# Layer 1's up projection as seven half-size block products, right operands summed and split once

## The chip, the cores and the metric

One core of a Trainium2 chip runs the whole program. The metric is the device time of one execution in microseconds. The engines are TensorE (PE, matmuls, with weight loads shown apart as PEld), VectorE (DVE), ScalarE (ACT), GpSimd (POOL) and SyncE (SP); here POOL and SP mostly issue DMA transfers. Each engine works off its own queue in order and waits on semaphores for the others.

## The reference

Two layers of a hybrid block over 1024 latent tokens (and 256 context tokens, which layer 1 reads but no longer updates), D = 1024, followed by a final norm. The change touches the feed-forward part of layer 1:

```python
def conv_ffn(h, w_up, conv_w, conv_b, w_down):
    u = dwconv(h @ w_up, conv_w, FFN_CONV // 2) + conv_b      # D_FF = 2816, w_up: D x 2*D_FF, 3 taps over tokens
    gate, val = jnp.split(u, 2, axis=-1)
    return (jax.nn.silu(gate) * val) @ w_down
...
        x = x + g1[:, None, :] * y_l
        x = x + g2[:, None, :] * conv_ffn(modulate(x, norm_ffn_g[layer], sh2, sc2), ffn_w_up[layer], ...)
    return rmsnorm(x, final_norm_g)
```

`modulate` is an RMS norm times (1 + scale) plus shift. Everything is float32.

## The kernel before

Activations lie transposed, channels on the 128 partitions and tokens along the row: x is eight tiles of 128x1024 (`xl`). A float32 product is made of three matmuls of fp32r operands. Each operand is split into a high part (ACT casts it, line 315) and a low part (DVE subtracts, line 316), and `mm3` (line 336) adds high x high, high x low and low x high in PSUM.

A layer is mixers, then `project_out` (the output projection, which adds onto x in two passes, first token half B0 and then B1), then `norm_block` for the two halves, `ffn_up` and `lat_down`. Tiles come from rings: 36 slots of 128x1024 (`L`), 8 of 128x512 (`H2`), two weight slots for raw loads (`wr`, `wd`, one each), two each for their high and low parts (`wh`, `wl`), in PSUM two tiles of two banks (tag a, `ps`) and four of one bank (tag b, `pb1`). A scheduler orders each engine's instructions, mostly in the order of the code, and puts in the waits; what it made of the code is fixed when the program is built.

`ffn_up` walks over 22 chunks of 128 channels, gate then value (`up(f, val)`, line 1260). One block loads 1024x128 weights (`wr`, 512 KB), splits them, and multiplies both token halves (`pu`, 2 x 24 matmuls of 128x512 on line 341). Then the three-tap convolution reads PSUM: ACT applies the middle tap and the bias (line 1275), DVE the two outer taps (1276, 1277). ACT makes Silu of the gate (1280), DVE multiplies (1220). In layer 0 the context tokens are a second job in the same loop (`puc`), with their own down projection `ctx_down` (`pd`, line 1253, added onto `xc`). The products are kept in SBUF (`bt`) or parked in DRAM (`act`, from GpSimd's queue, lines 1223 to 1230).

`lat_down` (line 1303) is already a product in seven block products of half size. Chunks of even and odd number are the two halves of the sum. Its seven stages take six pairs of chunks each, 24 matmuls a pair; operands for the next pair are made while one runs (`operands`, line 1429: `ah`/`al` from raw weight loads, `br`/`bd` or `rb`/`db` from activations `b`). Accumulators are `px` (tag a) and `py` (tag b). At the end of layer 1 `fin` normalises and stores the output.

## Time and profile before

| | |
|---|---|
| three runs | 3070.68, 3074.61, 3086.83 us; median 3074.61 |
| profiled run | 3071.11 us, of which the span 3069.0 |
| PE, DVE, ACT busy | 95%, 57%, 43% of the span |
| layer 1's first up-projection matmul to its last | about 2328 to 2816 us |
| layer 1's down projection to the end | about 2816 to 3069 us |

Times inside the run are microseconds from the span's start. A row of the timeline gives the start, the duration, engine, line, operation, output and input tiles (buffer numbers left out), and in brackets how long the engine sat idle before it and what ended that. "x3" is three such instructions in a row. A window row gives the stretch, then the busy time of each engine with the number of its instructions, the granted clock of PE (1.00 is full), the busy share of the DMA engines and GB/s.

### The profile page before, as it was taken

The page shows a single profiled execution, that of the slowest core. Times are in us where ns is not written, and L with a number is a line of the kernel's source. Part 1 is how long each engine was busy: PE and PEld are TensorE (multiplying, and loading weights), DVE is VectorE, ACT ScalarE, POOL GpSimd, SP SyncE. Part 2 cuts the span into 40 slices and gives each one's busy share as a digit, 9 for nine tenths or more (in the row PEclk, how much of TensorE's full clock was granted, in tenths as well). Part 3 has the DMA queues.
Part 4 walks back from the last instruction along what each step waited for, and adds up shares of the span by engine and source line. Part 5 has one row for each costly group of instructions (what it writes and reads, how often), then busy time and mean ns, then how long its engine had stood idle before and what let it go on. Part 6 is the DMA issues. An engine that isn't in the chain of part 4 may idle for free.

```text
span 3069.0 us, 41616 instructions
## 1 busy us (share of the span) xinstructions
PE 2925.5 (95%) x16472; PEld 2323.1 (76%) x16472; DVE 1764.7 (57%) x2746; ACT 1312.6 (43%) x2219; POOL 184.6 (6%) x284
## 2 busy tenths in 40 slices
PE   6999898989999999999999899998999999999998
PEld 5877675559888888888778787775577888887776
DVE  5466555665644444444686756767755444345775
ACT  5366754663422222222333555766744222223343
POOL 2000011010000000000111000011000000001010
PEclk8999999999999999999999999999999999999998
DMA  7221247333232232221575200123053222123672
GB/s 293 69 63 49 73 125 193 105 112 115 93 97 96 93 100 88 71 76 66 195 255 155 82 28 29 33 78 93 19 164 124 62 62 62 55 62 113 216 196 90
DMA packets 271571, 318.44 MB, mean 104 GB/s; under 512 B 18156, under 2 KB 199568, under 8 KB 271376
## 3 DMA queue, kind: packets, MB, share of 16 engines
q1 hardware_dynamic: 242928, 231.29, 24.2%
q0 software_dynamic: 28272, 84.43, 8.5%
q8 instruction: 130, 2.13, 0.3%
q14 instruction: 65, 0.53, 0.1%
q10 hardware_dynamic: 176, 0.07, 0.0%
HBM read 265.12 MB, written 50.59 MB: 103 GB/s over the span
## 4 chain that ended last, share of the span: by engine, by line
PE 82%; ACT 6%; DVE 6%; DMA 4%; issue 2%; SPq 0%; ACTq 0%; DVEq 0%; POOLq 0%
PE pu L341 31%; PE pl L341 9%; PE px L1457 7%; PE py L1457 4%; PE puc L341 4%; PE iv L587 3%; PE yo L1160 3%; PE sc L1005 3%; PE yo L1154 2%; PE pov L1047 2%; PE pc L341 2%; PE pt L1030 2%; PE pd L1253 2%; PE ada L199 2%; PE hd L668 2%
## 5 line engine op out<-in xcount | busy, mean ns | idle before, releaser
L341 PE MATMUL pu<-hh,wh 128*128 128x512 f32 x1408 | 555.8, 395 | 1.5 <-ACT u L1275 1.3
L341 PE MATMUL pu<-hh,wl 128*128 128x512 f32 x1408 | 552.2, 392 | 0.0
L341 PE MATMUL pu<-hl,wh 128*128 128x512 f32 x1408 | 548.6, 390 | 0.0
L315 ACT CAST wh<-wr 128x1024 fp32r<-128x1024 f32 x154 | 161.5, 1050 | 513.1 <-PE pu L341 277.4
L316 DVE TENSOR_TENSOR wl<-wr,wh 128x1024 fp32r<-128x1024 f32 x154 | 190.0, 1234 | 329.9 <-ACT wh L315 322.7
L341 PEld LDWEIGHTS pu<-hh,wh 128*128 128x128 f32 x1408 | 264.5, 188 | 66.9 <-issue 11.4
L341 PEld LDWEIGHTS pu<-hh,wl 128*128 128x128 f32 x1408 | 264.4, 188 | 60.0 <-issue 0.7
L341 PEld LDWEIGHTS pu<-hl,wh 128*128 128x128 f32 x1408 | 264.4, 188 | 57.8 <-issue 0.5
L1276 DVE SCALAR_TENSOR_TENSOR u<-pu,col_fcb,u 128x1023 f32<-128x1023 f32 x44 | 56.4, 1283 | 327.3 <-ACT u L1275 327.3
L341 PE MATMUL pl<-hh,wh 128*128 128x512 f32 x512 | 211.0, 412 | 2.2 <-ACT wh L315 1.0
L341 PE MATMUL pl<-hh,wl 128*128 128x512 f32 x512 | 206.0, 402 | 1.1 <-DVE wl L316 1.1
L341 PE MATMUL pl<-hl,wh 128*128 128x512 f32 x512 | 205.2, 401 | 0.0
L1275 ACT ACTIVATE u<-pu,col_nf,col_fcw 128x1024 f32<-128x1024 f32 x44 | 53.0, 1206 | 318.9 <-PE pu L341 318.9
L315 ACT CAST ah<-raw 128x512 fp32r<-128x512 f32 x132 | 76.2, 618 | 216.0 <-PE px L1457 102.6
L341 PEld LDWEIGHTS pl<-hh,wh 128*128 128x128 f32 x512 | 96.4, 188 | 35.3 <-issue 14.0
L316 DVE TENSOR_TENSOR al<-raw,ah 128x512 fp32r<-128x512 f32 x132 | 85.9, 688 | 59.5 <-ACT ah L315 56.2
L1011 DVE TENSOR_REDUCE st<-sc 128x1 f32<-128x641 f32 (+2 forms) x144 | 106.7, 745 | 17.1 <-ACT sc L1010 15.5
L341 PEld LDWEIGHTS pl<-hh,wl 128*128 128x128 f32 x512 | 96.5, 188 | 26.0 <-issue 5.1
L1014 ACT ACTIVATE pb<-sc,st 128x641 f32<-128x641 f32 (+2 forms) x144 | 106.3, 739 | 20.6 <-DVE st L1011 17.8
L341 PEld LDWEIGHTS pl<-hl,wh 128*128 128x128 f32 x512 | 96.7, 189 | 23.8 <-issue 6.3
L1277 DVE SCALAR_TENSOR_TENSOR u<-pu,col_fcw,u 128x1023 f32<-128x1023 f32 x88 | 112.8, 1283 | 3.0
L1005 PEld LDWEIGHTS sc<-kc,qt 128*128 128x128 f32 x288 | 44.0, 191 | 80.0 <-ACT pb L1014 35.9
(419 smaller groups left out, 6587.8 us busy)
## 6 DMA issues: line engine op xcount, KB each, us to landing
raw<-in_ffn_w_down_dram SPq DMA_DIRECT2D x220, 256.0 KB
aw<-in_ada_w_dram SPq DMA_DIRECT2D x96, 512.0 KB
wr<-in_ffn_w_up_dram SPq DMA_DIRECT2D x88, 512.0 KB
wr<-in_w_in_dram SPq DMA_DIRECT2D x34, 512.0 KB
wr<-in_w_out_dram SPq DMA_DIRECT2D x128, 128.0 KB
act<-u POOLq DMA_DIRECT2D x55, 256.0 KB, 4.2
b<-act POOLq DMA_DIRECT2D x25, 512.0 KB, 8.1
dr<-in_ffn_w_down_dram SPq DMA_DIRECT2D x22, 512.0 KB
```

What stands on the lines that cost most here:

```text
L199: PE.matmul(out=pt[32 * q:32 * q + 32, h0:h0 + 256], lhsT=cl[:, k, :], rhs=wr[:, q * 256:(q + 1) * 256], start=(i == 0), stop=(i == 2 * KT ...
L315: S.copy(out=hi, in_=raw)
L316: eng.tensor_tensor(out=lo, in0=raw, in1=hi.bitcast(F32), op=sub)
L341: PE.matmul(out=o, lhsT=wl[k] if pi == 2 else wh[k], rhs=hl[k] if pi == 1 else hh[k], start=(k == 0 and pi == 0), stop=(k == nk - 1 and pi ...
L587: PE.matmul(out=po[:, 0:384], lhsT=hh[1 if pi == 1 else 0][k][:, t0:t0 + P], rhs=wiv[k][1 if pi == 2 else 0], start=(k == 0 and pi == 0), ...
L668: PE.matmul(out=pv[64 * hf:64 * hf + 64, ci, :].rearrange("p (h t) -> p h t", h=2), lhsT=kw(ci, hf), rhs=z[:, :, b:b + 64], start=True, st ...
L1005: PE.matmul(out=o_, lhsT=qt[:, hh, :], rhs=k_[:, ksl], start=(pi == 0), stop=(pi == 1 and not ms))
L1011: V.tensor_reduce(out=st[:, 0, c_], in_=sc[:, s0:769], axis=mybir.AxisListType.X, op=ALU.min)
L1014: S.activation(out=pb, in_=sc[:, s0:769], func=AF.Exp, bias=st[:, 0, c_], scale=-1.0, accum_out=st[:, 1, c_])
L1160: PE.matmul(out=o, lhsT=wl[k] if pi == 2 else wh[k], rhs=a[1 if pi == 1 else 0][:, s_], start=False, stop=(ki == 3 and pi == 2), skip_grou ...
L1277: V.scalar_tensor_tensor(out=u[:, 0:n - 1], in0=pu[:, 1:n], scalar=cw(2), in1=u[:, 0:n - 1], op0=mult, op1=add)
L1457: PE.matmul(out=acc[m], lhsT=(al if pi == 2 else ah)[:, i, c_], rhs=(bl if pi == 1 else bh)[:, i, :], start=((isy or si == 0) and j == 0 a ...
```

## The change

Layer 1 leaves `ffn_up` (which is now layer 0's alone) and gets `ffn_up7`. One chunk f is taken as a 2x2 block product: rows are gate and value weights, the sum runs over two halves of D, columns are the two token halves. In a Winograd form this takes seven products of half the sum's length, 12 matmuls each, instead of eight. The products are numbered by their operands:

- left operands, per chunk: 1 and 2 are halves of the gate weights (`ug`), 4 a half of the value weights (`uv`); 5, 6 and 7 use DVE sums of them (`sums`: s1, s2, s3), and 3 uses s2 with a gate half added by an accumulating DMA from GpSimd's queue. Each is split into `sw` when it is made, three products ahead.
- right operands, once for all chunks: `B11`, `B21`, `B22` are normalised activations, `T1` to `T4` sums of them, made in place in x by `norm7` and `sums7` and split into 28 tiles `t7`. x itself is copied to DRAM (`xmid`) before it is overwritten.
- 1, 6, 5 and 3 add up in one half of a PSUM tile `ux`, which ACT copies out to SBUF after each (`cg`, `cv`); 2 goes to its other half and 7 and 4 to `uz`, which DVE adds to the copies. The convolution then reads SBUF.

Products of the activations are all parked in DRAM, (0, 0) too, and `lat_down` loads them back. In both layers the first operands of `lat_down` are now made before the last block of the up projection (`pre_`, `pre`).

```diff
-             for a, b in ((0, 1), (1, 0), (1, 1))} for l in range(DEPTH)]
+             for a in range(2) for b in range(2)} for l in range(DEPTH)]
...
+            if (f, val) == (NF - 1, 1):
+                pre_()
...
+    def norm7(xs, th, l, xm, tb):
...
+            G.dma_start(out=xm[:, k, sl], in_=x_)
+            hm = H2("hm")
+            V.scalar_tensor_tensor(out=hm, in0=x_, scalar=A_, in1=rs[0], op0=mult, op1=mult)
+            S.activation(out=x_, in_=hm, func=AF.Identity, bias=B_)
+            if th == 0:
+                tb["B11" if k < 4 else "B21"].append(both(x_))
...
+        def sums(f):
+            raws[f, "s1"], s4[f], raws[f, "s3"] = H2("s1"), H2("s2"), H2("s3")
+            V.tensor_tensor(out=raws[f, "s1"], in0=half(raws[f, 1], 0), in1=half(raws[f, 1], 1), op=add)
+            a11 = half(raws.pop((f, 0)), 0)
+            V.tensor_tensor(out=s4[f], in0=a11, in1=raws[f, "s1"], op=sub)
+            V.tensor_tensor(out=raws[f, "s3"], in0=a11, in1=half(raws[f, 1], 0), op=sub)
+            if f + 1 < NF:
+                load_g(f + 1)
...
+            split(half(t_, 0), half(t_, 1), raw)
+            ops[f, i] = half(t_, 0), half(t_, 1)
+            if i == 6:
+                G.dma_start(out=k4(raw), in_=cols(f, 0)[:, 4:8], accum_op=add)
+            if i == 4 and f + 1 < NF:
+                load_v(f + 1)
...
+        for f in range(NF):
+            seq += [(f, 6), (f, 7), (f, 5)] + [(f + 1, 1)] * (f > 0) + [(f, 3), (f, 4)] + [(f + 1, 2)] * (f > 0)
...
+        for n_, (f, i) in enumerate(seq):
+            if n_ == 4:
+                yield
+            if todo:
+                opnd(*todo.pop(0))
+            elif (f, i) == (NF - 1, 3):
+                pre()
...
+            for k in range(4):
+                for pi in range(3):
+                    PE.matmul(out=out, lhsT=(al if pi == 2 else ah)[:, k * P:(k + 1) * P], rhs=rhs[k][1 if pi == 1 else 0],
+                              start=(i in (1, 2, 7) and k == 0 and pi == 0), stop=(k == 3 and pi == 2), skip_group_check=True)
...
+            elif i == 5:
+                S.copy(out=half(cv[f], 1), in_=x_)
+                V.tensor_tensor(out=half(cv[f], 1), in0=half(cv[f], 1), in1=cz[f], op=add)
...
+    def sums7(xs, tb, norm):
...
+                t3 = H2("t3")
+                V.tensor_tensor(out=t3, in0=b22, in1=b12, op=sub)
+                V.tensor_tensor(out=b12, in0=b12, in1=b11, op=sub)
+                V.tensor_tensor(out=b11, in0=b12, in1=b22, op=sub)
+                tb["T2"].append(both(b11))
+                tb["T3"].append(both(t3))
+            tb["T1"] += [both(half(xs[k], 1)) for k in range(4)]
...
+        else:
+            n1 = norm7(xl, 1, l, xmid[l], tb)
+            run(n1, 1)
+            next(f_)
+            sums7(xl, tb, n1)
```

On PE, before, in the middle of layer 1's up projection a block is one run of high and low parts of eight tiles h into one `pu` half:

```order
L341 MATMUL pu<-hh_18800,wh 128x512
L341 MATMUL pu<-hl_18808,wh 128x512
L341 MATMUL pu<-hh_18800,wl 128x512
L341 MATMUL pu<-hh_18801,wh 128x512
L341 MATMUL pu<-hl_18809,wh 128x512
```

On PE, after, at the same place, one chunk's product 6 (right operand T2, tiles 19791 to 19845), then two groups of the next chunk's product 1 (B11, 19320 on), then product 5 (T1, 19851 on) into the PSUM half that 6 left:

```order
L1445 MATMUL ux<-t_19791,sw 128x512 x3
L1445 MATMUL ux<-t_19809,sw 128x512 x3
L1445 MATMUL ux<-t_19827,sw 128x512 x3
L1445 MATMUL ux<-t_19845,sw 128x512 x3
L1445 MATMUL ux<-t_19320,sw 128x512 x3
L1445 MATMUL ux<-t_19374,sw 128x512
L1445 MATMUL ux<-t_19851,sw 128x512 x3
L1445 MATMUL ux<-t_19854,sw 128x512 x3
```

Product 1's remaining eight matmuls stand behind product 5. On DVE, before, a chunk of this stage is weight splits, conv passes and products:

```order
L316 TENSOR_TENSOR wl<-wr,wh 128x1024
L1276 SCALAR_TENSOR_TENSOR u<-pu,col_fcw_1009,u 128x1023
L1277 SCALAR_TENSOR_TENSOR u<-pu,col_fcw_1015,u 128x1023
L1220 TENSOR_TENSOR b<-u 128x512
L1220 TENSOR_TENSOR u<-u 128x512
L1229 TENSOR_TENSOR u<-u 128x512
```

On DVE, after, from the second outer tap of the gate to the first weight sum (s, line 1352) of the next chunk but one; `uv` is the split of operand 4, which frees the value weights' buffer:

```order
L1410 SCALAR_TENSOR_TENSOR u<-cg,col_fcw_1027,u 128x1023
L316 TENSOR_TENSOR sw<-s_20909,sw 128x512
L1409 SCALAR_TENSOR_TENSOR u<-cv,col_fcw_1021,u 128x1023
L1453 TENSOR_TENSOR cg<-cg,ux 128x512
L1410 SCALAR_TENSOR_TENSOR u<-cv,col_fcw_1027,u 128x1023
L316 TENSOR_TENSOR sw<-ug,sw 128x512
L1422 TENSOR_TENSOR u<-u 128x1024
L316 TENSOR_TENSOR sw<-uv,sw 128x512
L1424 TENSOR_TENSOR ev<-u,ev 128x512
L316 TENSOR_TENSOR sw<-s_20910,sw 128x512
L1352 TENSOR_TENSOR s_21050<-uv 128x512
```

The next value load (SP's queue) thus stands behind both conv chains, and the first sum behind that load. On ACT, before, at the start of layer 1's stage the last normalisation passes of the second token half are followed by the weights' cast and the first conv:

```order
L286 ACTIVATE hh_18806<-hm,mod_91 128x512
L286 ACTIVATE hh_18807<-hm,mod_91 128x512
L315 CAST wh<-wr 128x1024
L1275 ACTIVATE u<-pu,col_fcb_995,col_fcw_1009 128x1024 x2
```

On ACT, after, at that place, the last six of the casts of T1, B22 and T4 and what follows them; the first `COPY cv` empties product 6 of chunk 0, the second product 5:

```order
L315 CAST t_19869<-x_18802 128x512
L315 CAST t_19872<-x_18803 128x512
L315 CAST t_19879<-x_18800 128x512
L315 CAST t_19882<-x_18801 128x512
L315 CAST t_19885<-x_18802 128x512
L315 CAST t_19888<-x_18803 128x512
L1457 COPY cv<-ux 128x512
L315 CAST sw<-uv 128x512
L1459 COPY cv<-ux 128x512
```

All twelve casts of those operands stand ahead of the copy.

## Rows read from the trace of the kernel before

**Rows 1.** Page: engines' busy time; the chain that ended last, by engine.

```profile
PE 2925.5 (95%) x16472; PEld 2323.1 (76%) x16472; DVE 1764.7 (57%) x2746; ACT 1312.6 (43%) x2219; POOL 184.6 (6%) x284
...
PE 82%; ACT 6%; DVE 6%; DMA 4%; issue 2%; SPq 0%; ACTq 0%; DVEq 0%; POOLq 0%
PE pu L341 31%; PE pl L341 9%; PE px L1457 7%; PE py L1457 4%; PE puc L341 4%; PE iv L587 3%; PE yo L1160 3%; PE sc L1005 3%; PE yo L1154 2%; PE pov L1047 2%; PE pc L341 2%; PE pt L1030 2%; PE pd L1253 2%; PE ada L199 2%; PE hd L668 2%
```

**Rows 2.** Windows of layer 1's up projection, and the turn behind it.

```profile
2400.00:2500.00 100.00, 100.00 (x438) 82.04 (x438) 42.30 (x41) 24.68 (x23) 2.14 (x4) 1.00 0.19 58
...
2818.00:2830.00 12.00, 7.55 (x22) 5.52 (x23) 8.38 (x9) 2.49 (x4) 5.20 (x9) 0.72 0.59 178
```

**Rows 3.** Timeline of ACT in that stage: two weight casts that follow each other.

```profile
2508.74 1.05 ACT L315 CAST wh<-wr 128x1024 fp32r<-128x1024 f32 x1 [5.01 <-PE pu L341]
...
2519.73 1.05 ACT L315 CAST wh<-wr 128x1024 fp32r<-128x1024 f32 x1 [8.83 <-PE pu L341]
```

**Rows 4.** Groups by line and shape: busy us, mean ns, idle us before.

```profile
L316 DVE TENSOR_TENSOR al<-raw,ah 128x512 fp32r<-128x512 f32 x132 | 85.9, 688 | 59.5 <-ACT ah L315 56.2 <-PE fo L1476 3.1
...
L315 ACT CAST ah<-raw 128x512 fp32r<-128x512 f32 x132 | 76.2, 618 | 216.0 <-PE px L1457 102.6 <-PE py L1457 98.4 <-PE pu L341 11.3
L1034 ACT COPY pts<-pt 128x512 f32<-128x512 f32 x128 | 74.4, 585 | 15.3 <-PE pt L1030 15.3
...
L1275 ACT ACTIVATE u<-pu,col_fcb,col_fcw 128x1024 f32<-128x1024 f32 x44 | 52.8, 1200 | 1.5 <-PE pu L341 1.5
...
L1174 DVE SCALAR_TENSOR_TENSOR x<-yo,mod,x 128x512 f32<-128x512 f32 x32 | 24.0, 750 | 60.5 <-PE yo L1160 60.5
...
L848 DVE SCALAR_TENSOR_TENSOR th<-rg,th 128x1024 f32<-128x1024 f32 x8 | 9.8, 1225 | 9.0 <-ACT rg L889 9.0
```

**Rows 5.** Timelines of PE, then DVE, where layer 1's up projection starts.

```profile
2327.79 0.39 PE L1160 MATMUL yo<-yh,wl 128*128 128x512 f32 x1
2333.03 1.09 PE L270 MATMUL pm<-sq,cft 128*128 128x512 f32 x2 [1.87 <-DVE sq L268]
2354.87 0.47 PE L341 MATMUL pu<-hh,wh 128*128 128x512 f32 x1 [1.34 <-ACT u L1275]
...
2338.13 2.08 DVE L285 SCALAR_TENSOR_TENSOR hm<-x,acol,rs 128x512 f32<-128x512 f32 x3
2358.11 0.69 DVE L1220 TENSOR_TENSOR u<-u 128x512 f32<-128x512 f32 x1
2358.72 1.22 DVE L316 TENSOR_TENSOR wl<-wr,wh 128x1024 fp32r<-128x1024 f32 x1
```

**Rows 6.** Timeline of PE at the turn to layer 1's down projection.

```profile
2816.17 0.40 PE L341 MATMUL pu<-hh,wl 128*128 128x512 f32 x1
...
2823.72 0.79 PE L1457 MATMUL px<-bd,ah 128*128 128x512 f32 x1 [1.61 <-DVE bd L316]
...
2827.30 0.46 PE L1457 MATMUL px<-br,ah 128*128 128x512 f32 x1
...
2830.58 0.40 PE L1457 MATMUL px<-rb,ah 128*128 128x512 f32 x1
```

**Rows 7.** Timeline of PE at the same turn in layer 0.

```profile
1484.14 0.47 PE L1253 MATMUL pd<-ac,dh 128*128 128x256 f32 x2 [1.07 <-DVE uc L1277]
...
1488.94 0.62 PE L1457 MATMUL px<-br,ah 128*128 128x512 f32 x2
1492.97 0.80 PE L1457 MATMUL px<-bd,ah 128*128 128x512 f32 x1 [3.40 <-DVE bd L316]
...
1499.68 0.40 PE L1457 MATMUL px<-rb,ah 128*128 128x512 f32 x1
```

**Rows 8.** Weight loads: issue ns min/median/max; SP's waits (total, times, longest); one landing.

```profile
L325 SPq DMA_DIRECT2D wr<-in_ffn_w_up_dram x44: 367/368/379, 2313.6 to 2785.7; - x44
...
SPq L325 <- DMA wr<-in_ffn_w_up_dram: 122.8, 35, 4.3
...
b<-act POOLq DMA_DIRECT2D x25, 512.0 KB, 8.1
```

More of the change, by code (lines that the diff above doesn't have):

```diff
@@ L1278, in up @@
                 if not val:
-                    with sact if last and f == NF - 1 else ExitStack():
-                        S.activation(out=u, in_=u, func=AF.Silu)
-                        if last and f == NF - 1:
-                            S.preload_act_table_set(LN_EXP)
+                    S.activation(out=u, in_=u, func=AF.Silu)
                 elif s_:
@@ L1301, in ffn_up, with half, step @@
         yield
+    def half(t_, b):
+        return t_[:, b * 512:b * 512 + 512]
+    def norm7(xs, th, l, xm, tb):
+        sl = (B0, B1)[th]
+        rs = []
+        def step(k):
+            A_ = acol[l, 1][:, 0, k:k + 1]
+            B_ = mod[l][:, 24 + k, 0:1]
+            x_ = xs[k][:, sl]
+            G.dma_start(out=xm[:, k, sl], in_=x_)
[4 more added lines that the diff above has]
+                tb["B11" if k < 4 else "B21"].append(both(x_))
+        return [lambda: rs.append(rstd_of(cuts(xs, sl), 512))] + [lambda k=k: step(k) for k in range(KT)]
@@ new lines, in sums7 @@
+    def sums7(xs, tb, norm):
+        if True:
+            for k in range(4):
+                norm[k]()
+                norm[4 + k]()
+                (b11, b12), (b21, b22) = ([half(xs[k_], b) for b in range(2)] for k_ in (k, k + 4))
+                t3 = H2("t3")
[5 more added lines that the diff above has]
+            tb["T1"] += [both(half(xs[k], 1)) for k in range(4)]
+            tb["B22"] += [both(half(xs[k + 4], 1)) for k in range(4)]
+            for k in range(4):
+                b21 = half(xs[k + 4], 0)
+                V.tensor_tensor(out=b21, in0=b21, in1=half(xs[k], 0), op=add)
+            tb["T4"] += [both(half(xs[k + 4], 0)) for k in range(4)]
@@ L1372, in b_p1 @@
         def b_p1(j):
-            load_b(0, 1, j)
-            if (1, 0, j) not in bt:
-                load_b(1, 0, j)
+            for q in ((0, 0), (0, 1), (1, 0)):
+                if (*q, j) not in bt:
+                    load_b(*q, j)
             return bt[0, 0, j]
@@ L1443, in lat_down @@
         ops = [operands(*todo[0])]
+        yield
+        for j in range(len(PAIRS)):
+            if (0, 0, j) not in bt:
+                load_b(0, 0, j)
         for q, (si, j) in enumerate(todo):
@@ L1523, in tile_dit @@
                 run(steps0, 1)
-        bt = {}
-        f_ = ffn_up(l, h2, h2c, xc, bt, not want)
+        fins, afters = [], []
+        d_ = lat_down(l, xmid[l], bt, lambda si, xa: afters[0](si, xa), fins)
+        f_ = ffn_up(l, h2, h2c, xc, bt, lambda: next(d_)) if want else ffn_up7(l, xl, tb, lambda: next(d_))
         next(f_)
         run(steps0)
-        run(norm_block(cuts(xl, B1), *h2, B1, l, 1, 0))
-        for k in range(KT):
-            G.dma_start(out=xmid[l][:, k, :], in_=xl[k])
         if want:
+            run(norm_block(cuts(xl, B1), *h2, B1, l, 1, 0))
+            for k in range(KT):
+                G.dma_start(out=xmid[l][:, k, :], in_=xl[k])
             run(norm_block(xc, *h2c, BC, l, 1, 1))
+        else:
+            n1 = norm7(xl, 1, l, xmid[l], tb)
+            run(n1, 1)
+            next(f_)
+            sums7(xl, tb, n1)
         next(f_)
-        fins = []
         if want:
@@ L1550, in tile_dit @@
             hn = []
-            lat_down(l, xmid[l], bt, after, fins)
+            afters.append(after)
+            next(d_)
             hl, hc = hn[0]
```

120 lines of the change are left out of this document (113 added, 7 removed).

## The prediction

> **What bounds the kernel now.** I read the page's shares and its chain of work first: TensorE (PE) is busy 95% of the span, 82% of the chain that ended last is PE, and line 341 on tile pu, the up projection of both layers, is the largest single part [rows 1]. Then the windows: in the middle of layer 1's up projection PE is busy the whole 100 us at full clock, while VectorE (DVE) has 42 and ScalarE (ACT) 25 [rows 2]. So this stage is as long as its matmuls. Their pace is read from ACT, which starts one weight cast per block of 48 matmuls: 2508.74 and 2519.73 [rows 3], 10.99 / 48 = 0.229 us per matmul. The matmul rows themselves say 0.39, since neighbours overlap in the pipe. What is to be seen is that nothing but fewer matmuls, or a shorter wait at a stage's edge, can make this stretch shorter.
>
> **What it removes.** Layer 1's up projection has 22 chunks x 2 (gate, value) x 2 token halves x 8 k-tiles x 3 terms = 2112 matmuls. Seven products of half size take 22 x 7 x 4 x 3 = 1848. 264 x 0.229 = **60.5 us** less PE work per run, all of it in a stretch where PE has no idle time.
>
> **What it adds in each chunk.** A chunk's 84 matmuls last 19.2 us. DVE now does seven low-half splits (0.69 each), three weight sums (0.69), three adds out of PSUM (0.75, priced by the 512-wide PSUM operation of line 1174), four conv passes (1.23, priced by line 848, whose inputs lie in SBUF) and about 1.7 of products and differences: 15.8 us, 83%. These durations overlap at back-to-back starts (the pass behind one of 128x512 starts 0.61 after it; three hm passes take 2.08), so the queue itself is occupied for about 14.3 us, 75%. ACT: seven casts (0.62), four PSUM copies (0.59), two conv passes (at most 1.20) and one Silu (as much): 10.3 us, 54% [rows 4, 5]. Neither is a bound by its sum.
>
> By its chains it is closer. Three must be held against 19.2 us.
> (a) Product 5 adds onto the same PSUM half that product 6 left, so it must wait for ACT's copy of it. The order puts four matmuls of the next chunk between them: 0.92 of cover. The chain is 0.39 (last matmul) + 0.04 + 0.59 + 0.06 - 0.23 = 0.85. Hidden, by less than 0.1.
> (b) The value weights have one buffer. Its next load can't be issued before DVE has split the fourth block of it, and in DVE's order that split stands behind both conv chains. Counted from the copy after product 3: copy, cast and gate conv on ACT 2.2; the four conv passes, two adds, three splits and the product on DVE 9.1; the load; then the first sum, an add, a split and the second sum 2.6; the cast of operand 6, 0.5, behind which the next copy stands on ACT. Without the load that is 14.4. A load of before takes SyncE 0.37 us to issue, and its queue then waits 122.8 / 35 = 3.5 us for it to land [rows 8]. Ring: 14.4 + 3.9 = **18.3 us**, against 19.2.
> (c) Splits are made three products ahead (8.2 us), enough for any of the above.
> So I take PE as the bound, with 3 us in all for late copies and odd chunks, whose three parked blocks share the DMA engines with the load; bounds 0 and 25 (below).
>
> **The start of the stage is the price.** Before, PE goes from the last output projection matmul at 2327.79 into B0's blocks and is idle 1.87 and 1.34 only [rows 5], since normalising the second token half is 8 pairs of passes. After, that stretch needs differences and sums of the normalised tiles and their splits before five of the seven products exist. On before's clock: four products that need only the first half (48 matmuls, 11 us) start at 2328.0. The second of these waits for the next gate load, and the squares behind it on ACT follow late: I put the mean-square matmul pm at 2335.0 instead of 2333.03. From it to the first hm before takes 5.1 us (2338.13); with a cast, a split and a PSUM add queued between, 6.7: hm at 2341.7. PE has then run out of work (2341.6). DVE's chain from there: 8 hm at 0.67, 16 sums at 0.60 to 0.72, 8 splits at 0.60, one add and one split, and about 0.7 of hops to ACT: 22.1 us, so T2 and T3 are complete at 2363.8. In ACT's order twelve more casts (T1, B22, T4; 0.52 each, 6.2 us) stand **ahead of the copy of product 6**, and product 5 waits for that copy: it starts at 2369.85. By then 72 matmuls are done, worth 16.5 us; 41.85 have passed: 25.3 lost, against 3.2 before. Net **22.1**. Product 5 then starts at the low clock, as the turn to the down projection does now, where after 7 us with three matmuls the granted clock is 0.72 and starts stand 0.43 apart until 2827.30 [rows 2, 6]: 8 x 0.2 = 1.7. In the first chunk nothing covers the copy between 5 and 3: 0.85. Together **24.7**. Bounds: 12 if DVE's sums keep up with hm and the casts slip between them, 34 if the accumulating load of operand 3's weights lands as late as b<-act (8.1, [rows 8]) and its cast, which stands ahead of the first hm's ACT pass, holds the chain up.
>
> In the last chunk no matmul of a next one covers the two copies: 2 x 0.85 = **1.7**.
>
> **The turn to the down projection, layer 1.** Before, both px tiles wait for pu's conv and br/bd: pair 0 runs from 2816.17 to 2830.58, 14.2 us after the last matmul's slot, for 5.5 of work [rows 6]. After, the PSUM of product 3 is free one product before the end and pair 0's operands are split before the last conv, so pair 0 is 5.5. But the first token half now comes back from DRAM, and DVE still owes the last chunk's passes: the splits of pair 1 end 7.5 us after the end (due 5.5) and those of pair 2 at 15.1 (due 13.0). 9.6 in all: gain **4.7**, between 0 and 9.
>
> **The turn in layer 0.** The call before the last block moves pair 0's splits ahead of eight xc updates. Before, px stops for 3.40 (bd) after its first two at 1488.94 and after pd has idled 1.07 for one result, and runs on at the low clock; pair 1 starts at 1499.68 [rows 7]. After, ten px matmuls (2.3 us) stand in the pd waits (1.07 and two shorter ones). pd ends near 1489.5 and, with fourteen more, pair 1 could start at 1492.7: 7 gained. DVE and the DMA engines then limit some of it (b loads land 8.1 us after issue, [rows 8]): **5**, between 2 and 7. If nothing came of it, the forecast rises by those 5.
>
> **The sum.** -60.5 + 24.7 + 1.7 + 3 - 4.7 - 5 = -40.8. The profiled span 3069.0 becomes 3028; that run took 3071.1, 2.1 more, so 3030. That run lies 3.5 under the median of the three; I leave the forecast at **3030**, 1.4% under the median. A difference under 0.5% (15 us) can't be told from none here.
>
> **Rivals.**
> - *The ring of (b) sets the pace.* For it: DVE's order, and park writes now travel with the load. Against: DMA is busy 0.2 in this stage [rows 2]. With a load of 6 us the period is 20.4: 21 x 1.2 = 25 more, 3055.
> - *The same ring, and slower than before.* It needs the load to land after more than 6.9 us (period 21.3, where 21 x 2.1 eats the gain with the allowance of 3). If it lands as b<-act does, 8.1 [rows 8], the period is 22.5: 21 x 3.3 = 70, less the 3: **3097**. Against: those loads travel in windows with the DMA engines full, this one doesn't.
> - *The copies are not hidden.* A half of PSUM that is read between products stalls the next by 0.85; if both of a chunk's (6 to 5, 5 to 3) did, 21 x 1.7 = 36, less the 3 of the allowance: 3063. Against: eight matmuls cover the second. The Trainium skill, "Perfetto Trace Analysis", section "Optimizing Tensor Performance", speaks for this rival: independent groups should rotate through PSUM banks, so that the evacuation of one overlaps the next group's matmuls, and this change lets five products share one bank. No row of before shows such a shared bank.
> - *The start costs half.* ACT and DVE work finer interleaved than I add up: 12 less, 3018.
>
> **How the numbers follow.** Forecast 0.55 (3022 to 3042), cheap start 0.15, paced ring 0.17, unhidden copies 0.07, slow ring 0.06. The range 3012 to 3058 leaves out the last two and the outer tails, some 0.2. Faster by over 0.5% (under 3059): the first two, and most of the paced ring, 0.84; same 0.10; slower 0.06.
>
> **What would show it.** Steady chunks 19.2 to 19.4 us apart (cast to cast of the same operand) with PE busy throughout; PE idle 20 to 25 us in all between the last yo and the second chunk, the longest wait before product 5, put down to the copy; after the last uz matmul px without a gap; in layer 0 no wait for bd. A regular PE wait for the copy in each chunk speaks for the third rival, a DVE wait for uv's load ahead of the first sum for the ring. The forecast is wrong if the chunks' period is above 20, or if the start lasts under 12 or over 34.

## The result, and the profile after

The changed kernel takes 3042.27 us (median of four runs, 3040.61 to 3045.27) against 3074.0 before (four runs; the forecast knew three of them, median 3074.61): a ratio of 0.9893, interval 0.9875 to 0.9912. The forecast was 3030 in a range of 3012 to 3058: right in sign and inside the range, with a gain of 31.7 us where 44.6 was forecast (from 3074.61 to 3030). The profiled run (3040.61, span 3038.8) is read against the profiled run of before (3071.11, span 3069.0) stage by stage. The borders are starts of matmuls in the two traces; the end of an up projection is its last start plus a slot of 0.23.

| stage | before | after | change forecast | change measured |
|---|---|---|---|---|
| start to layer 1's last yo matmul (holds layer 0's turn) | 2327.8 | 2322.8 | -5 | -5.0 |
| last yo to the end of the up projection | 488.61 | 459.02 | -31.1 | -29.6 |
| from there to the first py matmul (the turn) | 38.95 | 42.84 | -4.7 | **+3.9** |
| first py to the end | 213.6 | 214.1 | 0 | +0.5 |
| span | 3069.0 | 3038.8 | -40.8 | -30.2 |

So 8.6 of the 10.6 us that are missing lie in one term, the turn to layer 1's down projection. The page of after, to be held against [rows 1] (engines' busy time, then the chain that ended last by engine):

```profile
PE 2880.4 (95%) x16208; PEld 2275.7 (75%) x16208; DVE 1901.4 (63%) x3005; ACT 1421.5 (47%) x2445; POOL 236.6 (8%) x348
...
PE 76%; DVE 8%; ACT 7%; DMA 6%; issue 2%; SPq 0%; POOL 0%; ACTq 0%; DVEq 0%; POOLq 0%
```

264 matmuls are gone, PE's busy time fell by 45, DVE's rose by 137. The chain now leaves PE more often. The windows say where (after, columns as in [rows 2]: steady chunks, then the turn):

```profile
2400.00:2500.00 100.00, 100.00 (x437) 81.34 (x437) 75.63 (x100) 49.74 (x72) 13.25 (x17) 1.00 0.39 98
...
2782.00:2811.00 29.00, 19.42 (x74) 14.41 (x73) 17.27 (x19) 9.83 (x13) 9.89 (x18) 0.82 0.83 312
```

In the steady stretch PE is busy throughout and DVE at 76%, as summed (75%). In the turn PE has 19.4 of 29 us at a mean clock of 0.82, and the DMA engines are busy 0.83 of the time.

**The start of the stage.** PE's timeline of after, against [rows 5]:

```profile
2322.84 0.39 PE L1160 MATMUL yo<-yh,wl 128*128 128x512 f32 x1
...
2343.76 0.80 PE L1445 MATMUL ux<-t,sw 128*128 128x512 f32 x1 [6.62 <-ACT t L315]
...
2364.84 5.49 PE L1445 MATMUL ux<-t,sw 128*128 128x512 f32 x12 [4.21 <-ACT cv L1457]
2371.01 3.07 PE L1445 MATMUL ux<-t,sw 128*128 128x512 f32 x12 [0.68 <-ACT cv L1459]
```

ACT's timeline at the same place:

```profile
2357.98 6.33 ACT L315 CAST t<-x 128x512 fp32r<-128x512 f32 x12
2364.22 0.57 ACT L1457 COPY cv<-ux 128x512 f32<-128x512 f32 x1
```

Product 5 starts at 2364.84, 42.0 after the last yo matmul (forecast 42.06), and what it waits for is ACT's copy of product 6 behind twelve casts. The steps before it are on time as well: the first hm pass, which begins to normalise the second token half, starts 14.2 after the last yo matmul (forecast 13.9), and the last split of T2 and T3 ends at 36.0 (forecast 36.0). The low clock behind product 5's start cost more than forecast: 6.17 us from the first matmul of product 5 to the first of product 3, of which 2.75 is the full pace of twelve; 3.4 lost, 2.55 forecast for clock and copy.

Two signs of the prediction did not come as it wrote them. PE's idle time up to the second chunk is 16.6 us in all, not 20 to 25, and the longest wait, 6.62, stands before product 6, not before product 5. The loss up to product 5 is the forecast one all the same (42.0 less 16.5 for 72 matmuls is 25.5, forecast 25.3): the rest of it is matmuls of products 6 and 7, which run between the waits at a granted clock of 0.50, the lower of its two levels:

```profile
2344.00:2361.00 17.00, 12.75 (x24) 6.74 (x24) 16.90 (x28) 9.14 (x17) 0.00 (x0) 0.50 0.00 0
```

**The steady chunks.** The two value casts that follow each other (ACT, against [rows 3]) stand 19.27 apart, that is 84 x 0.229:

```profile
2437.90 0.62 ACT L315 CAST sw<-uv 128x512 fp32r<-128x512 f32 x1 [1.22 <-PE uz L1445]
...
2457.17 0.62 ACT L315 CAST sw<-uv 128x512 fp32r<-128x512 f32 x1 [1.22 <-PE uz L1445]
```

Two chunks of the 22 are 1.3 longer. Here is one of them. DVE's first sum of two chunks in turn, SP's two issues of the load that it waits for, and the PE matmul that came late:

```profile
2657.12 0.69 DVE L1352 TENSOR_TENSOR s<-uv 128x512 f32<-128x512 f32 x1 [2.66 <-DMA uv<-in_ffn_w_up_dram]
...
2678.49 0.69 DVE L1352 TENSOR_TENSOR s<-uv 128x512 f32<-128x512 f32 x1 [4.75 <-DMA uv<-in_ffn_w_up_dram]
```

```profile
2653.12 0.37 SPq L1348 DMA_DIRECT2D uv<-in_ffn_w_up_dram  x1
...
2672.23 0.37 SPq L1348 DMA_DIRECT2D uv<-in_ffn_w_up_dram  x1
```

```profile
2689.39 11.32 PE L1445 MATMUL ux<-t,sw 128*128 128x512 f32 x48 [0.98 <-DVE cg L1453]
```

From its issue to the sum that waits for it, the load takes 4.0 us in the first (2653.12 to 2657.12) and 6.26 in the second, and that chunk is 20.56 long, from a start of uz to the like start in the next. The ring (b) of the prediction, 14.4 and the load, gives 18.4 and 20.7: the rival "paced ring" came true in two chunks of 22.

Which loads are late can be read from the DMA queues. In chunks 2 to 20 an even chunk's load has one park of 256 KB beside it and takes 3.8 to 4.3 us; an odd chunk's has three and takes 4.6 to 5.0. Three parks instead of one thus go with some 0.7 more, and PE does not wait for it. Only the loads of chunks 17 and 20 take over 6 us (6.26 and 6.42; 20 has one park), and only in these two loads does a packet of 16 KB fall that the profile counts to a queue of kind "instruction" (it starts 3.0 and 3.7 us after the issue and takes 1.4 and 1.0). Of the DMA queues between 2672 and 2679, the row of that one (packets, MB, share of the engines' time):

```profile
q8 instruction: 1, 0.02, 1.3%
```

**The turn.** PE's timeline of after, against [rows 6]:

```profile
2779.12 2.91 PE L1445 MATMUL uz<-t,sw 128*128 128x512 f32 x12
...
2788.24 0.74 PE L1651 MATMUL px<-rb,ah 128*128 128x512 f32 x2 [0.72 <-ACT rb L315]
2789.50 0.50 PE L1651 MATMUL px<-db,ah 128*128 128x512 f32 x1 [0.52 <-DVE db L316]
...
2797.72 1.22 PE L1651 MATMUL px<-br,ah 128*128 128x512 f32 x2 [2.94 <-ACT br L315]
2804.33 0.80 PE L1651 MATMUL px<-bd,ah 128*128 128x512 f32 x1 [5.39 <-DVE bd L316]
```

Pair 0 follows the last uz matmul without a gap, and pair 1 is as late as forecast (splits 7.6 us after the end, forecast 7.5). Pair 2 is not: its split ends 22.4 after the end, forecast 15.1. The chain of work in order of time (start, duration, engine, tile and line; "issue" is the step between two) names what held it:

```profile
2789.37 1.23 DVE u L1422
2790.59 0.28 issue
2790.88 0.44 POOL act L1426
...
2794.06 7.84 DMA b<-act
2801.89 0.02 issue
2801.92 0.04 DVE b L1519
2801.95 1.11 issue
2803.06 1.23 DVE bd L316
2804.29 0.04 issue
2804.33 10.89 PE px L1651 x40
```

The last chunk's product (line 1422) releases its park on GpSimd's queue. Behind the parks stand two loads of x and then the load of block (0,1) of pair 1. A sum of the *second* stage (line 1519) needs that block, and it stands on DVE **ahead** of pair 2's split of the *first* stage (`bd`). DVE's rows show it; the order was fixed when the program was built, so it could have been read before the run:

```profile
2796.76 1.23 DVE L316 TENSOR_TENSOR db<-b,rb 128x1024 fp32r<-128x1024 f32 x1 [0.17 <-ACT rb L315]
2801.92 1.22 DVE L1519 TENSOR_TENSOR b<-b 128x1024 f32<-128x1024 f32 x1 [3.94 <-DMA b<-act]
2803.06 1.22 DVE L316 TENSOR_TENSOR bd<-b,br 128x1024 fp32r<-128x1024 f32 x1
```

**Layer 0's turn.** Against [rows 7], pair 1 starts at 1491.47 instead of 1499.68, and no px waits 3.4 for bd:

```profile
1491.47 0.40 PE L1651 MATMUL px<-rb,ah 128*128 128x512 f32 x1
...
1497.94 0.50 PE L1651 MATMUL px<-bd,ah 128*128 128x512 f32 x1 [0.58 <-DVE bd L316]
```

### The profile page after: what moved, and what is told of

It is laid out like the page before. It is cut to its first block, busy times and chain, and to the rows that moved or that the text cites. A ratio compares the mean times of both kernels' runs of the same rounds, so it can differ in the third digit from the quotient of the medians.

```text
span 3038.8 us, 41813 instructions
## 1 busy us (share of the span) xinstructions
PE 2880.4 (95%) x16208; PEld 2275.7 (75%) x16208; DVE 1901.4 (63%) x3005; ACT 1421.5 (47%) x2445; POOL 236.6 (8%) x348
## 4 chain that ended last, share of the span: by engine, by line
PE 76%; DVE 8%; ACT 7%; DMA 6%; issue 2%; SPq 0%; POOL 0%; ACTq 0%; DVEq 0%; POOLq 0%
PE pu L341 16%; PE pl L341 9%; PE ux L1445 8%; PE px L1651 5%; PE py L1651 4%; PE puc L341 4%; PE uz L1445 3%; PE iv L587 3%; PE yo L1160 3%; PE sc L1005 3%; PE yo L1154 2%; DMA raw<-in_ffn_w_down_dram 2%; PE pov L1047 2%; PE pt L1030 2%; PE pc L341 2%
## 5 line engine op out<-in xcount | busy, mean ns | idle before, releaser
L1445 PE MATMUL ux<-t,sw 128*128 128x512 f32 x1320 | 320.6, 399 | 20.1 <-ACT t L315 10.5
L1445 PEld LDWEIGHTS ux<-t,sw 128*128 128x128 f32 x1320 | 248.3, 190 | 85.3 <-ACT t L315 13.1
L341 PE MATMUL pu<-hh,wh 128*128 128x512 f32 x704 | 278.7, 396 | 0.1
L341 PE MATMUL pu<-hh,wl 128*128 128x512 f32 x704 | 276.3, 393 | 0.0
L341 PE MATMUL pu<-hl,wh 128*128 128x512 f32 x704 | 275.1, 391 | 0.0
L341 PEld LDWEIGHTS pu<-hh,wh 128*128 128x128 f32 x704 | 132.2, 188 | 38.3 <-issue 11.4
L341 PEld LDWEIGHTS pu<-hh,wl 128*128 128x128 f32 x704 | 132.3, 188 | 29.0 <-issue 0.4
L341 PEld LDWEIGHTS pu<-hl,wh 128*128 128x128 f32 x704 | 132.2, 188 | 28.0 <-issue 0.2
L1445 PE MATMUL uz<-t,sw 128*128 128x512 f32 x528 | 132.6, 398 | 0.0
L1445 PEld LDWEIGHTS uz<-t,sw 128*128 128x128 f32 x528 | 100.6, 191 | 23.4 <-ACT t L315 0.9
L1014 ACT ACTIVATE pb<-sc,st 128x641 f32<-128x641 f32 (+2 forms) x144 | 106.3, 739 | 20.7 <-DVE st L1011 18.0
```

What stands on the lines that cost most here:

```text
L341: PE.matmul(out=o, lhsT=wl[k] if pi == 2 else wh[k], rhs=hl[k] if pi == 1 else hh[k], start=(k == 0 and pi == 0), stop=(k == nk - 1 and pi ...
L1014: S.activation(out=pb, in_=sc[:, s0:769], func=AF.Exp, bias=st[:, 0, c_], scale=-1.0, accum_out=st[:, 1, c_])
L1445: PE.matmul(out=out, lhsT=(al if pi == 2 else ah)[:, k * P:(k + 1) * P], rhs=rhs[k][1 if pi == 1 else 0], start=(i in (1, 2, 7) and k == 0 ...
```

## The experiments

Twelve kernels, each an edit of the changed one. All were read by the same borders (us):

| kernel | last yo to last uz start | end of uz to first py | first py to end | layer 0: last pd to first py | span |
|---|---|---|---|---|---|
| changed kernel | 458.8 | 42.8 | 214.1 | 29.6 | 3038.8 |
| e2_order | 457.4 | 32.1 | 209.1 | 32.8 | 3027.9 |
| e1_no_early | 458.0 | 47.7 | 214.9 | 36.2 | 3054.9 |
| e4_five_behind_six | 474.8 | 42.9 | 216.3 | 31.2 | 3064.2 |
| e3_load_twice | 519.5 | 44.3 | 215.8 | 31.0 | 3105.4 |
| e5_late_casts | 461.0 | 43.1 | 217.5 | 32.5 | 3045.8 |
| e6_no_sums | 438.7 | 43.9 | 215.0 | 29.0 | 3024.2 |
| e7_late_pool | 464.6 | 42.7 | 215.9 | 30.0 | 3047.8 |
| e10_order_first | 457.6 | 43.3 | 216.2 | 30.4 | 3042.6 |
| e8_order_last | 461.7 | 32.1 | 208.4 | 30.3 | 3022.7 |
| e9_order_both | 461.7 | 32.0 | 208.6 | 28.5 | 3022.4 |
| e11_order_both_only | 458.1 | 32.0 | 209.6 | 28.6 | 3016.7 |
| e12_loads_first | 457.7 | 39.1 | 214.4 | 31.3 | 3037.7 |

Nine of the twelve were run once; e8_order_last, e9_order_both and e11_order_both_only four or five times. Four runs of the changed kernel differ by 4.7 us, and between these kernels the last yo matmul lies anywhere from 2317 to 2334, which the edits explain only in small part (6.6 of it is e1_no_early's layer 0). So the columns are compared, not the spans.

**e2_order: the order of the operands.** The theory is that the turn is late because of what stands ahead on ACT and DVE; the rival, that 19 blocks must come back from DRAM. `oact` and `odve` make ACT and DVE keep the order of the code.

```diff
+        oact, odve = InOrder(tc, ACT_ENGINE), InOrder(tc, mybir.EngineType.DVE)
...
         def operands(si, j):
+            if l == DEPTH - 1 and si < 2:
+                with oact, odve:
+                    return operands_(si, j)
+            return operands_(si, j)
+
+        def operands_(si, j):
```

> The changed kernel with one edit: in layer 1's down projection ACT and DVE must take the operands of the first two stages in the order of the pairs. In the changed kernel the casts of pair 3 stand ahead of those of pair 2 on ACT, and on DVE a sum of the second stage (line 1519) that waits 3.94 us for a load stands ahead of pair 2's split. Theory 'order': the gaps of 2.94 and 5.39 us before pair 2 (starts 2797.72 and 2804.33) go, and most of the low clock behind them (seven starts 0.2 us longer): 8 to 10 us less, span about 3030, the first py matmul 31 to 34 us after the last uz matmul instead of 42.8. Rival 'bytes': the DMA engines bring 19 blocks of 512 KB back at 410 GB/s, and pair 2 waits for them in any order: less than 2 us gained, span 3037 to 3039.

Measured: 32.1 for the turn, 10.8 less, and only pair 1's short waits are left (PE):

```profile
2793.14 0.73 PE L1658 MATMUL px<-rb,ah 128*128 128x512 f32 x2 [0.72 <-ACT rb L315]
2794.39 0.50 PE L1658 MATMUL px<-db,ah 128*128 128x512 f32 x1 [0.53 <-DVE db L316]
```

The order theory holds; with the same blocks to load, bytes are not the bound. The turn is now 6.9 shorter than before the change: with the pairs in order, the forecast gain of 4.7 is there, and more. First py to the end fell by 5.0 as well, which the expectation did not have.

**e10_order_first: which half of the order.** The same with `si < 1`: pairs in order in the first stage, the second stage free.

> As the kernel with ordered operands, but ACT and DVE keep the order of the pairs in the first stage of layer 1's down projection only; the second stage's sums and splits are free again. The kernel ordered in both stages had two gains over the changed kernel: 10.8 us between the last uz and the first py matmul (32.0 against 42.8), and 5.0 between there and the end (209.1 against 214.1). Theory: the first is the pair order of the first stage, the second that of the second stage; so here 32 to 33 and 213 to 215. Rival: the later gain follows from the earlier start of the loads alone; then 32 to 33 and 209 to 210.

Measured: 43.3 and 216.2. For the turn both were wrong, and that settles it: the order of the pairs alone gives nothing. The sum of the second stage still stands ahead of a split of the first, and DVE sits idle 9.92 us until that sum's block lands:

```profile
2803.49 1.23 DVE L1519 TENSOR_TENSOR b<-b 128x1024 f32<-128x1024 f32 x1 [9.92 <-DMA b<-act]
2804.63 1.22 DVE L316 TENSOR_TENSOR bd<-b,br 128x1024 fp32r<-128x1024 f32 x1
```

The gain behind the turn is gone too, so both gains hang on the second stage's order. The second stage ordered alone was not run.

**e12_loads_first: the load instead of the order.** The loads stand in the code ahead of the last parks, the operands' order is the scheduler's.

```diff
         ops = [operands(*todo[0])]
+        if l == DEPTH - 1:
+            for j in range(1, len(PAIRS)):
+                load_b(0, 0, j)
+            for j in range(1, 4):
+                load_b(0, 1, j)
         yield
```

> The changed kernel with one edit: in layer 1 the loads of the blocks (0,0) and of the first three (0,1) of the down projection stand in the code ahead of the last chunk's parks, so that GpSimd's queue issues them before it waits for DVE's last product; the operands' order is the scheduler's again. Theory: the lost time is DVE waiting, with a sum of the second stage at the head of its queue, for a load that GpSimd issued behind the last parks; with the load early the sum may stay where it is, and from the last uz to the first py matmul it takes 32 to 36 instead of 42.8. Rival (the DMA engines are full at 410 GB/s until 2811 whatever is issued first, and the order alone cured it because it asked for less at once): 40 to 43.

Measured: 39.1, between the two. The sum no longer waits, but the order came out differently once more: the last chunk's conv passes and pair 3's casts now stand ahead of pair 2's cast on ACT, and PE waits for that (ACT, then PE):

```profile
2799.51 2.94 ACT L315 CAST br<-b 128x1024 fp32r<-128x1024 f32 x3
```

```profile
2800.60 1.22 PE L1656 MATMUL px<-br,ah 128*128 128x512 f32 x2 [5.26 <-ACT br L315]
```

An early load takes away one of the two things that met, a late load and a pass out of order; the other found a new place.

**e1_no_early: without the early operands.** `pre_` and `pre` do nothing, and the first operands are made behind the last block in both layers.

```diff
-        f_ = ffn_up(l, h2, h2c, xc, bt, lambda: next(d_)) if want else ffn_up7(l, xl, tb, lambda: next(d_))
+        f_ = ffn_up(l, h2, h2c, xc, bt, lambda: None) if want else ffn_up7(l, xl, tb, lambda: None)
...
             next(d_)
+            next(d_)
...
+            next(d_)
             next(d_)
```

> The changed kernel without the early first operands of the down projections, in both layers (they are made behind the last block, as in the kernel before). The two layers are read apart in the trace. Layer 0: theory of the prediction, the early operands are worth 5: the first py matmul of layer 0 comes 5 to 6 us later than the 1517.74 of the changed kernel; rival, the earlier start comes from elsewhere: no change. Layer 1: theory 'queue' (the loads of the blocks stand behind the last parks on GpSimd's queue, issued 9 us after the last product and 8 us on the way): px starts 17 to 21 us after the last uz matmul, and the first py matmul comes 6 to 10 us later; rival 'bytes' (the stretch is as long as the transfers take): the first py matmul moves by less than 3. Span 3050 to 3055 by the first of each.

Measured: layer 0 36.2, as before (35.6). The ten kernels that have the early operands in layer 0 in the scheduler's order lie between 29.0 and 32.8, mean 30.8. Against the mean of the two kernels without them (35.9) they are worth 5.1, forecast 5; against this run alone the changed kernel has 6.6. Layer 1: 47.7, 4.9 later, between the two theories. The first pair's loads stood ahead of the last park after all, so px began 6.4 after the end, not 17 to 21; pair 2 waited until 2815.58. Early operands do gain in layer 1, and the order of pair 2 takes more than they give.

**e4_five_behind_six: a copy without cover.** PE's order of a chunk is fixed to 7, 6, 5 from chunk 2 on, so that nothing stands between 6 and 5.

```diff
-            seq += [(f, 6), (f, 7), (f, 5)] + [(f + 1, 1)] * (f > 0) + [(f, 3), (f, 4)] + [(f + 1, 2)] * (f > 0)
+            seq += [(f, 7), (f, 6), (f, 5)] + [(f + 1, 1)] * (f > 0) + [(f, 3), (f, 4)] + [(f + 1, 2)] * (f > 0)
...
+            with ope if 1 < f else ExitStack():
```

> The changed kernel with PE's order in each chunk fixed to 7, 6, 5, 1 of the next, 3, 4, 2 of the next, from chunk 2 on: nothing stands between product 6 and product 5 that adds onto the same PSUM half, where the changed kernel has four matmuls. Theory (a copy that nothing covers costs 0.84, as the three of the last chunk do: start to start 1.07 instead of 0.23): 20 chunks x 0.84 = 17 us more, span 3056. Rival (the copy is hidden by the pipe or by later slack in the chunk): period still 19.26, span 3039 within 3.

Measured: 16.0 more in the stretch, a chunk 20.19 instead of 19.27, with the same wait each time (PE, two chunks in turn):

```profile
2511.44 8.52 PE L1447 MATMUL ux<-t,sw 128*128 128x512 f32 x36 [0.67 <-ACT cv L1459]
...
2531.63 8.53 PE L1447 MATMUL ux<-t,sw 128*128 128x512 f32 x36 [0.68 <-ACT cv L1459]
```

So an uncovered copy, 0.85 in the prediction, costs 0.84 at the matmul that waits (1.07 start to start instead of 0.23). The start behind it comes after 0.34 instead of 0.23, and per chunk it is 0.92. Four matmuls (0.92) do hide the copy. (Twenty chunks at 0.92 are 18.4; the two late loads of the changed kernel, 2.6 us, cost nothing here.) The rule of the Trainium skill that the prediction weighed ("Perfetto Trace Analysis", section "Optimizing Tensor Performance": rotate banks so that an evacuation overlaps the next group's matmuls) holds here as a rule of cover: products 1, 6, 5 and 3 share one half of `ux`, and the time is lost only where no other group's matmuls stand between. (The prediction says five; product 2 goes to the other half.)

**e3_load_twice: the ring.** The value weights are loaded twice into their one buffer.

```diff
-            nc.sync.dma_start(out=k8(raws[f, 1]), in_=cols(f, 1))
+            for _ in range(2 if f else 1):
+                nc.sync.dma_start(out=k8(raws[f, 1]), in_=cols(f, 1))
```

> The changed kernel with the value weights loaded twice, one transfer after the other, into their one buffer, in chunks 1 to 21; nothing else differs. It lengthens the one step of the ring (b) by a load of 3 to 4 us. Theory of the prediction, ring 18.3 of a period of 19.26: the ring becomes 21.5 to 22.5, and 20 chunks x 2.3 to 3.2 = 45 to 65 us are lost, span 3085 to 3105. Rival, the splits made three products ahead absorb it (slack of 8 us): period still 19.26, span 3039 to 3042.

Measured: 60.7 more. PE now waits for operands in chunk after chunk:

```profile
2513.17 0.74 PE L1446 MATMUL uz<-t,sw 128*128 128x512 f32 x2 [1.80 <-ACT sw L315]
2514.48 2.33 PE L1446 MATMUL uz<-t,sw 128*128 128x512 f32 x9 [0.57 <-DVE sw L316]
...
2535.23 2.34 PE L1446 MATMUL uz<-t,sw 128*128 128x512 f32 x9 [1.21 <-DVE sw L316]
```

The ring is real and less than one load's length under the period. That splits are made three products ahead absorbs nothing, since the load itself waits for the last of them.

**e6_no_sums: the price of the start.**

```diff
-                t3 = H2("t3")
...
-                tb["T3"].append(both(t3))
-            tb["T1"] += [both(half(xs[k], 1)) for k in range(4)]
+            tb["T2"] += tb["B11"]
+            tb["T3"] += tb["B21"]
+            tb["T1"] += tb["B11"]
...
+            tb["T4"] += tb["B21"]
```

> The changed kernel without the differences and sums of the right operands: products 6 and 5 multiply B11, products 7 and 4 multiply B21, and only B22 is made of the second token half. It leaves out 16 DVE sums and 16 splits; the number of matmuls is the same. It prices the start. Theory of the prediction (the start costs 25 against 3 before, nearly all by DVE's chain of sums and splits): the stretch from the last yo to the last uz matmul falls by 19 to 23 us, from 458.8 to 436 to 440. Rival (the wait for the mean square and the low clock carry it, and come back in any form): it falls by less than 12.

Measured: 20.1 less. PE's waits of that start after the products of the first half are 3.48 and 0.68 (against 6.62, 1.05, 2.32, 0.51, 4.21 and 0.68). The sums and splits make 20.1 of the 23.8 that the prediction summed for the start (22.1 of net loss and 1.7 of clock). The edit also leaves out ACT's casts for these 16 operands, so it does not tell DVE's share from ACT's.

**e5_late_casts: the copy ahead of the casts.** B22 and T4 are split behind products 6 and 7 of chunk 0, which come where the new `yield` stands.

```diff
-            if n_ == 4:
+            if n_ in (4, 6):
                 yield
...
             tb["T1"] += [both(half(xs[k], 1)) for k in range(4)]
+            yield
             tb["B22"] += [both(half(xs[k + 4], 1)) for k in range(4)]
```

> The changed kernel with one edit at the start of the stage: the operands B22 and T4 are split behind products 6 and 7 of chunk 0 in the order of the code, so that ACT's copy of product 6 has only T1's four casts ahead of it, not twelve. Theory of the prediction (product 5 waits for that copy, not for its operands): product 5 starts 38.5 to 39 us after the last yo matmul instead of 42.0, and the stretch from the last yo to the last uz matmul falls from 458.8 to about 455.5. Rival (the splits of T1, B22 and T4 on DVE are the next limit): product 5 starts as early, but products 3 and 4 wait for their operands and less than 1 us remains of it.

Measured: product 5 starts at 38.3 as expected, and the stretch is 2.2 *longer*. Neither theory has the reason. Matmul by matmul, counted from the last yo, this kernel leads the changed one by 3.7 at product 5 and still by 3.6 when 286 of the stage's matmuls have started, 92 us after the last yo. Then one wait turns the lead into 2.7 behind. The chain of work that ended last puts it down to chunk 3's value load (the chain, then DVE, then PE):

```profile
2402.51 7.01 DMA uv<-in_ffn_w_up_dram
```

```profile
2409.54 0.69 DVE L1352 TENSOR_TENSOR s<-uv 128x512 f32<-128x512 f32 x1 [4.95 <-DMA uv<-in_ffn_w_up_dram]
```

```profile
2419.36 14.08 PE L1445 MATMUL ux<-t,sw 128*128 128x512 f32 x48 [3.21 <-DVE cg L1453]
```

DVE has been idle 4.95 us when that sum starts, so at that point it owed no splits. Behind PE's wait the granted clock is 0.54 for 6.7 us (2419.3 to 2426), and that is nearly the other half of the loss (2.9 of 6.3). In the changed kernel the same load takes 4.58 and none of this happens. Here a 16 KB packet of the "instruction" queue falls into it, as into the late loads of chunks 17 and 20. So the run does not show that the rival won: with a load of 4.6 the chain would end 2.4 earlier, and about 1 us of the wait and most of the lead would stay (an estimate from these rows; no run shows it).

**e7_late_pool: sums on GpSimd.** As e5_late_casts, with eight of the 16 sums on GpSimd.

```diff
-                V.tensor_tensor(out=t3, in0=b22, in1=b12, op=sub)
+                G.tensor_tensor(out=t3, in0=b22, in1=b12, op=sub)
...
-                V.tensor_tensor(out=b21, in0=b21, in1=half(xs[k], 0), op=add)
+                G.tensor_tensor(out=b21, in0=b21, in1=half(xs[k], 0), op=add)
```

> The kernel with the late casts of B22 and T4, and besides eight of the 16 sums of the right operands (T3's differences and T4's sums) on GpSimd instead of DVE, where a like pass takes 1.3 us. Theory (DVE's queue, one pass per 0.61, sets the pace of the tiles of T2 and T3): 7 of them stand ahead of the last tiles, 4.3 us less; product 5 starts 34.5 to 36 us after the last yo matmul, the stretch to the last uz matmul 451 to 452. Rival (ACT's passes and the hops between engines set the pace, or GpSimd's pass is late): within 1 us of the kernel with the late casts alone, 455.5.

Measured: product 5 at 41.1, the stretch 464.6; worse than either theory. Of the 464.6, 6.4 are the same late load of chunk 3 (6.91 us, and PE's wait of 3.12 behind it); up to there this kernel leads the changed one by 0.3, where e5_late_casts leads by 3.6. So the sums on GpSimd cost 3.3 instead of gaining. DVE's splits beside a GpSimd pass take 1.65 to 1.77 us instead of 0.68 (POOL, then DVE):

```profile
2345.12 1.72 POOL L1491 TENSOR_TENSOR x<-x,x 128x512 f32<-128x512 f32 x1 [2.07 <-DVE x L1483]
2346.80 1.73 POOL L1481 TENSOR_TENSOR t<-x,x 128x512 f32<-128x512 f32 x1
```

```profile
2345.74 1.65 DVE L316 TENSOR_TENSOR t<-x,t 128x512 fp32r<-128x512 f32 x1
2347.31 1.77 DVE L316 TENSOR_TENSOR t<-t,t 128x512 fp32r<-128x512 f32 x1
```

**e8_order_last, e9_order_both, e11_order_both_only: a better version.** e8_order_last is e2_order with PE's order of the last chunk fixed to 6, 7, 5, 3, 4; e9_order_both keeps the operands' order in layer 0 too (`si < 2` without the condition on l); e11_order_both_only is e9_order_both without the fixed last chunk.

> The changed kernel with the operands of the first two stages of layer 1's down projection in the order of the pairs (as before), and PE's order in the last chunk fixed to 6, 7, 5, 3, 4, so that 7 covers the copy of 6. Theory: 10.8 + 5.0 of the order and 0.84 of the covered copy, less what layer 0's turn scatters from run to run (2 to 3): 3024 to 3030, ratio to the kernel before 0.983 to 0.987. Rival: what the one look showed was scatter of the stretch from py to the end, then 3030 to 3034.

> The same with the operands' order kept in layer 0's down projection as well. Theory: layer 0 has the same inversion, since its second pair's split waits 0.6 to 2.9 us for a load: 1 to 3 us less than the kernel with layer 1 alone. Rival: the order takes pair 1's splits back behind the last chunk's context passes, where the early operands had put them ahead, and layer 0 loses 1 to 5.

> The changed kernel with the operands of the first two stages in the order of the pairs in both layers' down projections, and PE's order of the last chunk as the scheduler had it. In the two kernels with the last chunk reordered the stretch from the last yo to the last uz matmul was 461.7, against 457.4 with the operands' order alone: product 6 ahead of 7 waited 3.6 us for DVE's add of product 2. Theory: that comes back, and nothing else: stretch 457 to 459, from the last uz to the first py matmul 32, from there to the end 208 to 209; 3019 to 3022, ratio to the kernel before 0.982 to 0.984. Rival (the stall moves elsewhere, or the ordered layer 0 had been a lucky run): 3023 to 3030.

Measured: e8_order_last 3028.84 (ratio to before 0.9856, interval 0.984 to 0.9872), e9_order_both 3023.71 (0.9839, 0.9823 to 0.9856), e11_order_both_only **3019.30** (median of five, 0.9825, 0.981 to 0.9841). The fixed last chunk was a loss: the copy is covered, but product 6, now ahead of 7, waits for DVE's add of product 2 (e8_order_last, PE):

```profile
2765.78 4.59 PE L1447 MATMUL ux<-t,sw 128*128 128x512 f32 x12 [3.61 <-DVE cg L1455]
```

Taking it out again gave 3.6 back. With order in layer 0 its turn is 28.5 and 28.6, 2.3 under the mean of the others, but only 0.5 under the shortest of them; that gain is not shown beyond the scatter. The last kernel beats both: 23 us under the changed kernel's median. Of the 22.1 between the two spans in the table, 10.8 lie in layer 1's turn and 4.5 behind it, which the order explains, and 0.7 in the up projection; 6.1 lie ahead of the last yo, where layer 0's turn makes 1.0 and the rest is not explained by the edit.

## Why the prediction was right, and where it was off

- **The matmuls.** Right. Steady chunks 19.27 apart, forecast 19.2 to 19.4.
- **The start.** Right in its steps up to product 5 (42.0, forecast 42.06), which the copy behind the casts holds; clock and copy 3.4 instead of 2.55 (and its 8 x 0.2 is 1.6, not 1.7). Wrong in two signs: it put the whole loss down as idle time, and a good part of it is matmuls at a clock of 0.50. e6_no_sums puts the price at 20.1 above a start without sums. The rival "cheap start" had nothing for it as the kernel stands; e5_late_casts shows that eight of the casts ahead of the copy made 3.7 of it at product 5.
- **Copies and ring.** (a) Right: hidden by four matmuls, 0.84 where not (0.92 with the start behind it). (b) Right in its sum: a load of 4.0 leaves the ring under the period, 4.6 to 5.0 in the odd chunks brings it to the edge (19.0 to 19.4), and over 6 puts it above in two chunks, 2.6 us in all, inside the 3 that were allowed. What makes these two late was not in the text: it named the parks. The last chunk's two copies: 1.07 start to start, 0.84 lost each, forecast 0.85.
- **Layer 0's turn.** Right: 5.1 over ten kernels, forecast 5. They scatter by 3.8, so the agreement to 0.1 is luck.
- **Layer 1's turn.** This is the step that failed: "the splits of pair 1 end 7.5 us after the end [...] and those of pair 2 at 15.1 (due 13.0)", a gain of 4.7 "between 0 and 9". It became a loss of 3.9, outside its own bounds. The first half was right (7.6). The second counted DVE's passes and left out that one of them, the second stage's sum, waits for a load (7.84) that GpSimd could issue only after the last chunk's product, parks and two loads of x. Counted as the chain has it: the product ends 8.7 after the end, 3.5 pass until the load is issued at 2794.06, 7.8 until it lands, 1.2 with the sum, 1.2 with the split: 22.4. That the order was at fault, and not the number of blocks to be loaded, is shown by e2_order (turn 32.1); that the order of the pairs without that of the second stage does not cure it, by e10_order_first. The term names DVE's passes and the blocks that come back from DRAM; GpSimd's queue, which issues those loads behind the parks, stands in no step of it.
- **The rest.** The profiled run lies 1.8 above its span and 1.7 under the median of the four. The total fell inside the range although the turn left its own bounds: the range was drawn for the ring and the start, and that it also covered a miss in a third term is luck.

The loads of chunks 17 and 20 are late in every one of these kernels but e3_load_twice and e4_five_behind_six, whose chunks are longer. The packets of the "instruction" queue come some 29 us apart in this stage, about one and a half chunks, so that they meet the 4 to 5 us of a load only now and then. Over the changed kernel and the eleven of its edits that load once, chunks 2 to 20 give 228 value loads. The 199 without such a packet took 3.7 to 5.2 us; of the 29 with one, 24 took 5.5 to 7.0, and five, all in e4_five_behind_six, 3.8 to 4.9. That the packet makes the load late is not shown by an edit, and why those five were not late stays open.

## What to carry to other kernels

A scheduler that may put the next stage's work early can put it at the head of an in-order queue, ahead of work that is due; look in the order for a pass whose input comes from another queue, and count that queue's chain, not only the pass. A term for a turn between two stages needs all queues written down, the one that issues the transfers above all. Before an edit is called a loss, follow its lead along the stage, matmul by matmul: one late load can take in one place what the edit had gained and kept for 50 us.

## What the hardware showed that was not expected

- DVE's subtraction of two SBUF operands (128x512) takes 0.68 us alone and 1.65 to 1.77 beside a GpSimd pass on SBUF; each ends 0.55 after the GpSimd pass ends (2346.84 and 2347.39; 2348.53 and 2349.08), as if it began only then (spans on GpSimd are rough in these profiles). The Trainium skill ("SBUF — State Buffer", section "SBUF: two separate sides") says that DVE and GpSimd share a port pair as an exclusive lock, and that the loser waits for the whole instruction; the trace agrees with it.
- The same load of 512 KB on SP's queue takes 3.8 to 5.0 us in most of chunks 2 to 20, from its issue to the sum that waits for it, and 6.26 and 6.42 in two (chunks 17 and 20), with the DMA engines as a whole busy 0.4. One or three parks of 256 KB beside it make 0.7 of difference. The late ones are those into which a 16 KB packet of the "instruction" queue falls, here and in eleven other kernels (24 of 29 such loads took 5.5 us or more, none of 199 others took over 5.2).
